# Five pairs of the convolution's input projection as seven half-size products, with their block sums on VectorE and later splitting of the early weight pieces

## The chip, the cores and the metric

One core of a Trainium2 chip runs the kernel. The metric is the device time of one execution in microseconds (us), taken as the median of repeated runs; lower is better.

## The reference

A decoder trunk on 512 tokens of width 1024, with one layer of each of two kinds. What the change touches is the first mixer, ahead of everything else:

```python
def short_conv_mixer(h, w_in, conv_w, w_out):
    b_gate, c_gate, u = jnp.split(h @ w_in, 3, axis=-1)   # h: 512 x 1024, w_in: 1024 x 3072
    v = c_gate * u
    vp = jnp.pad(v, ((0, 0), (CONV_WIDTH - 1, 0), (0, 0)))
    conv = sum(conv_w[k] * vp[:, k:k + S] for k in range(CONV_WIDTH))
    return (b_gate * conv) @ w_out                        # w_out: 1024 x 1024
```

Behind it come a squared-ReLU MLP (1024 to 4096 and back), a shared key/value side, sparse attention, a second MLP and a last RMS norm.

## The kernel before

Everything is float32 outside and float16 in the matrix products: each operand is split into a high half and a low half (`whi`, `wlo` for weights, `x_98` or `xs` for activations), and a product is three matmuls, high by high, low by high and high by low, all added up in PSUM. Activations lie with their 1024 channels on partitions, as eight chunks of 128 x 512 tokens.

Weights stream in as pieces of 128 x 1024 values. SP issues the load into one of three `wst` buffers, ACT writes `whi`, DVE writes `wlo`, each into one of four buffers, and TensorE (PE) uses them some microseconds later. `convert_piece` does this in the order of the list `pieces`; `ahead` keeps a given number of pieces converted before they are used.

The input projection goes in four groups p of 256 channels. In each group three parts (the gate c, the values u, the gate b, as `pc`, `pu`, `pb`) are one pair each: two PSUM banks of 128 x 512, eight chunks, three terms, so 48 matmuls of 512 columns, done by `pair`. PSUM has two banks each of `a`, `b` and `c`; pairs take them in turn as a,b then b,c then c,a. Behind each pair DVE and ACT make `cv_t`, `cv_v`, `cv_o` and `cv_b` of it and at last the convolution's output `y`, again as two halves. The output projection is four more pairs on `y`, each followed by the residual `X`, its sum of squares `ssacc` and the next input `xs`.

Some weights that attention needs much later are split during this stage: `split_some` loads a piece as `pre_in`, makes both halves as `pre_hl`, and SP stores them to DRAM as `early`. There are 14 such pieces, one for each pair from the second group on until all are done.

The whole stage, from the first load to the last output pair, is recorded first and then issued by a planner (`Plan`): a list scheduler that gives each engine a fixed order by its own estimates. On the chip every engine works through its order one by one and waits where an operand is not there; so an instruction that waits holds back all that stand behind it on its engine. Behind the stage comes the MLP, which already uses the seven-product form in its second projection: a 2 x 2 block product with seven block products in place of eight, on sums of blocks (`W_SUMS` for the weights, `R_SUMS` for the activations, `PRODUCTS` for the pairs of blocks). Helper lines L241 (the planned stages) and L275 (the MLPs) stand for nearly all instructions in the profile, so that they are told apart by their tiles.

Of the kernel before, what the change touches and what calls it, by code (L numbers as in the profile page):

```python
# [10 lines left out]
F32 = mybir.dt.float32  # L11
# [269 lines left out]
def body(ctx, tc, x, rel_bias, norm_mix, norm_mlp, mlp_w1, mlp_w2, a_w_in, a_conv_w, a_w_out,  # L281
# [42 lines left out]
    def up_pair(w, m):  # L324

        v = w.rearrange("(c p) (j m n) -> p c j m n", p=128, j=2, n=128)
        for k in (0, 4):
            pieces.append((v[:, k:k + 4, :, m, :], (4, 256), SW))

    def down_blocks(w, p, half):  # L330

        v = w.rearrange("(j c p) n -> c p j n", j=2, p=128)
        for c in range(8 * half, 8 * half + 8, 2):
            pieces.append(([v[c + k, :, :, p * 256:(p + 1) * 256] for k in range(2)], None, SW2))
# [11 lines left out]
            cols(w, c0, 256, scale, k, 4)  # L346


    v = a_w_in[0].rearrange("(c p) (s n) -> c p s n", p=128, s=3)
    for c in range(8):  # L350
        pieces.append((v[c, :, :, 0:256], (3, 256), SW))
    for p in range(1, 4):
        for part in (1, 2, 0):
            block(a_w_in[0], part * D + p * 256)
    for p in range(4):
        block(a_w_out[0], p * 256)
    mlp_pieces(0)
# [3 lines left out]
    CMPS = [(55, 0, 0), (58, 0, 1), (61, 0, 2), (62, 0, 3), (77, 1, 0), (78, 1, 1), (85, 1, 3), (89, 1, 2)]  # L361
    LEAD_IN = ["k0", "q0"]

    RATE = 1
    PRE = ["raw1", "phi0", "q2", "cmp", "q3"]
    early, early_out = [], {}

# [25 lines left out]
    mlp_pieces(1)  # L393

    NS, NW, AHEAD = 3, 4, 2
    NS2, NW2, AHEAD2, PIECE2 = 3, 4, 3, 2048


    W_SUMS = ((OP.add, 4, 0, 2), (OP.subtract, 5, 4, 1), (OP.subtract, 6, 1, 0), (OP.subtract, 7, 3, 5))
# [9 lines left out]
    def load_piece(first=None):  # L409
        i = pos["dma"]  # L410
        if i >= len(pieces):
            return
        if i in early:
            pos["dma"] += 1
            return
        src, shape, _ = pieces[i]
        if shape is None:
            t = wk[0].tile([128, PIECE2], F32, name="wst2", bufs=NS2)
            for k, u in enumerate(src):
                SPQ.dma_start(t[:, k * PIECE:k * PIECE + 512].rearrange("p (j n) -> p j n", j=2), u)  # L420
        else:
            t = wpool.tile([128, PIECE], F32, name="wst", bufs=NS)
            a, n = shape
            v = t[:, :a * n].rearrange("p (a n) -> p a n", a=a)
            if len(src.shape) == 4:
                v = v.rearrange("p a (j n) -> p a j n", j=2)
                for j in range(2):
                    SPQ.dma_start(v[:, :, j], src[:, :, j])
            elif first:
                for k in (1, 2, 0):  # L430
                    (first if k == 1 else SPQ).dma_start(v[:, k], src[:, k])
            else:
                SPQ.dma_start(v, src)
        staged[i] = t
        pos["dma"] += 1

    def convert_piece(step=1024):
# [12 lines left out]
            yield  # L450
        elif shape is None:
            b = t.rearrange("p (k b n) -> p k b n", k=2, n=128)
            with tc.issue_after(root_op[0].ins):
                for e, o, x, y in W_SUMS:
                    DVE.tensor_tensor(b[:, :, o], b[:, :, x], b[:, :, y], op=e)
            hi, lo = (wk[0].tile([128, 2, 7, 128], F16, name=n, bufs=NW2) for n in ("whi2", "wlo2"))
            ACT.activation(hi, b[:, :, 1:], AF.Copy, scale=sc)
            DVE.scalar_tensor_tensor(lo, b[:, :, 1:], sc, hi, op0=OP.mult, op1=OP.subtract)
            ready[i] = (hi, lo)
            yield  # L460
        else:
# [10 lines left out]
            ready[i] = (r(hi), r(lo))  # L472
        while pos["dma"] < len(pieces):
            like = [j for j in range(pos["cv"], pos["dma"]) if blocked(j) == blocked(pos["dma"]) and j not in early]
            if len(like) >= (NS2 if blocked(pos["dma"]) else NS):
                break
            load_piece()

# [18 lines left out]
                pass  # L497
        return ready.pop(i)

    def ahead(far=AHEAD2):  # L500
        while pos["cv"] < len(pieces) and pos["cv"] < pos["use"] + (far if blocked(pos["cv"]) else AHEAD):
            yield from convert_piece()

    def drain(gen):
# [174 lines left out]
    def x_rstd():  # L679
        ss0 = work.tile([128, 4], F32, name="ss0")  # L680
        for t in range(4):
            junk = wk[0].tile([128, D], F32, name="junk", bufs=1)
            ACT.activation(junk, xt[t], AF.Square, accum_out=ss0[:, t:t + 1])
        return rstd_of(ss0)


    ys = new_split(wk[0], "y")
    for p in range(4):
        pc, pu, pb = [], [], []
        if p == 0:  # L690
# [35 lines left out]
            rb2 = ftile("rb2", 1)  # L726
            DVE.tensor_tensor(rb2, rby, rby, op=OP.mult)
            ws = [next_piece(), next_piece()]
        if p == 1:
            ext = wk[0].tile([H, EXT], F32, name="ext")  # L730
            POOL.memset(ext[:, 0:PAD], NEG)
# [7 lines left out]
            for i in range(2):  # L739
                PE.transpose(pp[:, i * 16:(i + 1) * 16], pe_in[:, i], ident[0:16, 0:16])  # L740
            ACT.activation(pet.rearrange("p a b -> p (a b)"), pp[:, 0:32], AF.Copy)
        for dst in (pc, pu, pb):
            if p:
                dst += [acc(), acc()]
                pair(xs, dst)
            else:
                for k in range(2):
                    first_pairs(dst, ws[k], 6 + k)
            drain(ahead())
            split_some(RATE if p else 0)  # L750
# [928 lines left out]
```

## Time and profile before

| | |
|---|---|
| median of 3 runs | 1102.13 us (1101.77 to 1102.78) |
| the profiled execution's own time | 1103.79 us |
| its span, first to last instruction | 1102.0 us |
| granted TensorE clock, mean | 0.999 |
| input projection, second to fourth group | 44.7 to 137.9 us |
| output projection | 137.9 to 179.3 us |
| first MLP begins | 179.4 us |

The profile is one execution. Busy time of an engine is the time in which an instruction ran on it; for PE, matmuls overlap in the pipeline, so their rate is read from the distance of their starts and not from their length. A row of the timeline gives the start, the length, the engine, the line, what it writes and reads, and in brackets the idle time ahead of it with what ended it.

### The profile page before, as it was taken

What the parts mean: (1) busy time and instruction counts of PE and PEld (TensorE: products, weight loads), DVE (VectorE), ACT (ScalarE), POOL (GpSimd) and SP (SyncE); (2) the same over time, 40 slices, a digit from 0 to 9 for tenths busy, and PEclk for the clock granted to TensorE, in tenths of its full rate; (3) what the DMA queues carried; (4) which work ended last, traced back from release to release, by engine and by line L of the source; (5) the groups of instructions that cost most, each with busy time, mean ns of one, the idle gap of its engine ahead of it and who ended that gap; (6) DMA issues with size and microseconds to landing.
All of it is one profiled execution on the core that took longest, in us unless ns stands there. A gap on an engine that the chain in (4) does not pass through costs nothing.

```text
span 1102.0 us, 20132 instructions
## 1 busy us (share of the span) xinstructions
PE 1088.4 (99%) x8009; PEld 696.0 (63%) x8009; DVE 864.5 (78%) x1594; ACT 564.7 (51%) x892; POOL 60.2 (5%) x89
## 2 busy tenths in 40 slices
PE   9999999999999999999999999999999999999997
PEld 4444444446885447885856686675444788444897
DVE  5977466986898776979677779997898799865776
ACT  6544244644333444527666677865655434343353
POOL 1000000000000000000011022211000000000021
PEclk9999999999999999999999999999999999999999
DMA  7897335543333332304424361002753333330232
GB/s 239 283 310 246 112 99 153 153 128 90 119 105 115 115 96 75 99 20 143 139 80 134 78 206 64 21 21 58 208 156 110 108 109 116 115 96 1 77 97 78
DMA packets 155615, 131.37 MB, mean 119 GB/s; under 512 B 8332, under 2 KB 147296, under 8 KB 155520
## 3 DMA queue, kind: packets, MB, share of 16 engines
q1 hardware_dynamic: 152672, 124.74, 37.0%
q10 hardware_dynamic: 2464, 4.70, 1.3%
q8 instruction: 63, 1.03, 0.4%
q0 software_dynamic: 384, 0.63, 0.2%
q14 instruction: 32, 0.26, 0.1%
HBM read 117.56 MB, written 9.48 MB: 115 GB/s over the span
## 4 chain that ended last, share of the span: by engine, by line
PE 93%; DVE 3%; ACT 1%; DMA 1%; issue 1%; POOL 0%; SPq 0%; POOLq 0%; DVEq 0%; ACTq 0%
PE c L275 19%; PE b L275 17%; PE a L241 16%; PE a L275 15%; PE c L241 9%; PE b L241 9%; PE d L275 4%; PE d L241 2%; PE e L275 2%; DVE at_s L241 1%; PE e L241 1%; DVE at_pl L241 0%; DMA whi<-early 0%; ACT xq L241 0%; DMA wst<-a_w_in_dram 0%
## 5 line engine op out<-in xcount | busy, mean ns | idle before, releaser
L275 PEld LDWEIGHTS <-whi 128*128 128x128 f16 x2784 | 272.4, 98 | 139.9 <-issue 0.2
L275 ACT ACTIVATE whi<-wst 128x1024 f16<-128x1024 f32 (+1 forms) x126 | 173.2, 1380 | 199.0 <-PE b L275 70.5
L275 DVE SCALAR_TENSOR_TENSOR wlo<-wst,whi 128x1024 f16<-128x1024 f32 (+1 forms) x126 | 204.3, 1624 | 17.0 <-ACT whi L275 16.6
L275 PEld LDWEIGHTS <-wlo 128*128 128x128 f16 x1392 | 136.2, 98 | 70.8
L241 PEld LDWEIGHTS <-whi 128*128 128x128 f16 x1024 | 97.3, 98 | 96.0 <-issue 2.7
L275 PE MATMUL b<-xs,whi 128*128 128x512 f16 x384 | 114.3, 379 | 0.0
L275 PE MATMUL c<-xs,whi 128*128 128x512 f16 x384 | 114.2, 379 | 0.0
L275 DVE TENSOR_TENSOR wst<-wst 128x256 f32<-128x256 f32 x256 | 95.9, 420 | 21.6 <-DMA wst<-mlp_w_dram 20.5
L275 DVE TENSOR_TENSOR rl<-ml_z,rh 128x1792 f16<-128x1792 f32 x32 | 64.7, 2023 | 43.7 <-ACT rh L275 43.7
L241 ACT ACTIVATE whi<-wst 128x512 f16<-128x512 f32 (+5 forms) x85 | 63.4, 765 | 69.0 <-PE a L241 19.2
L241 DVE SCALAR_TENSOR_TENSOR wlo<-wst,whi 128x512 f16<-128x512 f32 (+5 forms) x85 | 72.3, 863 | 23.4 <-ACT whi L241 23.2
L241 ACT ACTIVATE at_p<-at_s,at_m 128x128 f32<-128x128 f32 (+3 forms) x128 | 71.1, 556 | 35.5 <-DVE at_m L241 33.8
L241 PEld LDWEIGHTS <-wlo 128*128 128x128 f16 x512 | 50.2, 98 | 51.5
L275 ACT ACTIVATE rh<-ml_z 128x1792 f16<-128x1792 f32 x32 | 54.3, 1696 | 54.5 <-DVE ml_z L275 54.5
L275 PE MATMUL a<-xs,whi 128*128 128x512 f16 x256 | 76.1, 379 | 0.0
L275 PE MATMUL c<-xs,wlo 128*128 128x512 f16 x192 | 72.8, 379 | 0.0
L275 PE MATMUL b<-xs,wlo 128*128 128x512 f16 x192 | 72.8, 379 | 0.0
L241 DVE CUSTOM_DVE_ANT_0 at_s<-b,T 128x128 f32<-128x128 f32 (+3 forms) x128 | 59.3, 485 | 16.5 <-PE b L241 15.6
L275 PE MATMUL a<-rh,wlo 128*128 128x256 f16 x256 | 69.1, 273 | 0.0
L275 PE MATMUL a<-rh,whi 128*128 128x256 f16 x256 | 69.1, 273 | 0.0
L275 PE MATMUL a<-rl,whi 128*128 128x256 f16 x256 | 67.8, 273 | 0.0
L275 PE MATMUL c<-rh,wlo 128*128 128x256 f16 x248 | 67.6, 273 | 0.0
(264 smaller groups left out, 2173.7 us busy)
## 6 DMA issues: line engine op xcount, KB each, us to landing
wst<-mlp_w_dram SPq DMA_DIRECT2D x256, 256.0 KB, 3.5
wst<-a_w_in_dram SPq DMA_DIRECT2D x18, 512.0 KB, 6.0
early<-pre_hl SPq DMA_DIRECT2D x14, 512.0 KB, 4.8
wst<-w_kv_dram SPq DMA_DIRECT2D x10, 512.0 KB, 3.7
T<-ext_d ACTq DMA_DIRECT2D x4, 1056.0 KB, 7.0
wst<-a_w_out_dram SPq DMA_DIRECT2D x8, 512.0 KB, 3.5
wst<-b_w_o_dram SPq DMA_DIRECT2D x8, 512.0 KB, 3.8
whi<-early SPq DMA_DIRECT2D x14, 256.0 KB, 3.6
```

Of the source, the lines that this page charges most:

```text
L241: getattr(self.engines[t["e"]], t["op"])(*t["args"], **t["kw"])
L275: return real(*args, **kwargs)
```

## The change

The pairs (group, part) in `SEVEN` (part 1 is `pc`, 2 is `pu`, 0 is `pb`) are computed by a new function `seven`. It views the 1024 x 256 weights and the 1024 x 512 activations as 2 x 2 blocks, and makes seven products of four chunks, three terms and 256 columns each: 84 matmuls of 256 columns in place of 48 of 512. It needs:

- weight pieces in the two-chunk form `wst2` (two buffers), four `W_SUMS` additions of 256 values each, and a split of seven blocks, 2 x 896 values, in place of 1024;
- sums of blocks of the activations, once for all five pairs (`block_sums`, four calls, tiles `sv_z` and the new `xs` in this stage);
- the combination of the seven products in three PSUM banks: ACT copies product 0 from bank `a` to bank `b` as a start for further products there, and copies two partial sums to `sv_p` and `sv_u`; DVE adds these (`sv_d<-c`, `sv_d<-b`), ACT copies the other two halves of `sv_d`. The operations that used to read a pair from PSUM read `sv_d`.

The early pieces are recorded in other places: one behind pair (2, 0), and three, three, four and the rest behind the four output pairs (`PACE`, `PACE_OUT`). `y` now lies in the buffer of `xt`, and the squares of the input go to the `pre_in` buffers. The settings for the MLPs' blocks stay as they were.

```diff
+    SEVEN = [(2, 1), (2, 0), (3, 1), (3, 2), (3, 0)]
...
-            block(a_w_in[0], part * D + p * 256)
+            (seven_blocks if (p, part) in SEVEN else block)(a_w_in[0], part * D + p * 256)
...
-    RATE = 1
+    PACE = {(2, 0): 1}
+    PACE_OUT = [3, 3, 4, 99]
+    SUM_AT = {(0, 0): (0,), (1, 1): (1,), (1, 2): (2, 3,)}
...
+    AHEAD2 = {(SW, False): AHEAD, (SW, True): 2, (SW2, True): 3}
+    NS2 = {SW: 2, SW2: 3}
...
-            ACT.activation(hi, b[:, :, 1:], AF.Copy, scale=sc)
-            DVE.scalar_tensor_tensor(lo, b[:, :, 1:], sc, hi, op0=OP.mult, op1=OP.subtract)
+            for k in [slice(n, n + 1) for n in range(2)] if sc == SW else [slice(0, 2)]:
+                ACT.activation(hi[:, k], b[:, k, 1:], AF.Copy, scale=sc)
+                DVE.scalar_tensor_tensor(lo[:, k], b[:, k, 1:], sc, hi[:, k], op0=OP.mult, op1=OP.subtract)
...
+    def block_sums(c):
+        z = wk[0].tile([128, 8, 256], F32, name="sv_z", bufs=1)
+        for k in range(2):
+            g = vec[:, gain["mix0"] + 2 * c + k:gain["mix0"] + 2 * c + k + 1]
+            ACT.activation(z[:, 2 * k:2 * k + 2].rearrange("p a n -> p (a n)"), X[:, 2 * c + k], AF.Copy, scale=g)
+        for e, o, a, b in R_SUMS:
+            DVE.tensor_tensor(z[:, o], z[:, a], z[:, b], op=e)
+        ACT.activation(sums[:, 0, c], z[:, 4:8], AF.Copy)
+        DVE.tensor_tensor(sums[:, 1, c], z[:, 4:8], sums[:, 0, c], op=OP.subtract)
+
+    def seven(d):
+        X_, W_, V_ = (bank(g)[:, 0:256] for g in "abc")
+        ws = [next_piece(), next_piece()]
+        cv = ahead()
+
+        def product(i, ps, more=False):
+            a, b = PRODUCTS[i]
+            for c in range(4):
+                wh, wl = (u[:, c % 2, a - 1] for u in ws[c // 2])
+                xh, xl = (block_of(hl, c, b) for hl in range(2))
+                PE.matmul(ps, wh, xh, start=c == 0 and not more, stop=False, skip_group_check=more)
+                PE.matmul(ps, wl, xh, start=False, stop=False, skip_group_check=more)
+                PE.matmul(ps, wh, xl, start=False, stop=c == 3, skip_group_check=more)
+
+        u2, u5 = (wk[0].tile([128, 256], F32, name=n, bufs=1) for n in ("sv_u", "sv_p"))
+        lo, hi = slice(0, 256), slice(256, 512)
+        product(0, X_)
+        ACT.activation(W_, X_, AF.Copy)
+        product(4, V_)
+        ACT.activation(u5, V_, AF.Copy)
+        next(cv, None)
+        product(2, W_, True)
+        ACT.activation(u2, W_, AF.Copy)
+        product(5, V_, True)
+        DVE.tensor_tensor(d[:, 1, lo], V_, u2, op=OP.add)
+        next(cv, None)
+        product(3, W_, True)
+        DVE.tensor_tensor(d[:, 0, lo], W_, u5, op=OP.add)
+        product(1, X_, True)
+        ACT.activation(d[:, 1, hi], X_, AF.Copy)
+        drain(cv)
+        product(6, W_, True)
+        ACT.activation(d[:, 0, hi], W_, AF.Copy)
...
+            if (p, part) in SEVEN:
+                d = wk[0].tile([128, 2, S], F32, name="sv_d", bufs=2)
+                seven(d)
+                dst += [d[:, 0], d[:, 1]]
...
-            split_some(RATE if p else 0)
+            split_some(PACE.get((p, part), 0))
+            for c in SUM_AT.get((p, part), ()):
+                block_sums(c)
...
-        split_some(RATE if p < 3 else 99)
+        split_some(PACE_OUT[p])
```

The first place is PE in the fourth group. Before, a pair there runs as matmuls of 512 columns over two banks (`x_98` is the split input):

```order
L241 LDWEIGHTS whi
L241 MATMUL c<-x_98,whi 128x512
L241 LDWEIGHTS wlo
L241 MATMUL c<-x_98,wlo 128x512
L241 LDWEIGHTS whi
L241 MATMUL b<-x_98,whi 128x512
```

Now pair (3, 1) stands there as products of 256 columns; `whi_209` and `whi_212` are its own two weight pieces, `whi_223` is the first of the next pair (3, 2), and `xs` are the block sums of the activations:

```order
L241 MATMUL c<-xs,wlo_213 128x256
L241 LDWEIGHTS whi_212
L241 MATMUL c<-xs,whi_212 128x256
L241 LDWEIGHTS whi_223
L241 MATMUL a<-x_98,whi_223 128x256
L241 LDWEIGHTS whi_209
L241 MATMUL b<-xs,whi_209 128x256
L241 LDWEIGHTS wlo_210
L241 MATMUL b<-xs,wlo_210 128x256
```

The matmuls are of half the width, and the planner put one of the next pair between product 4 (bank `c`) and product 2 (bank `b`, which waits for ACT's copy).

The second place is DVE from the end of the third group on. Before, `cv_b` and `y` of that group were followed by one weight split for each half pair:

```order
L241 TENSOR_TENSOR cv_b<-c,rb 128x512
L241 TENSOR_TENSOR cv_b<-cv_b,cv_o 128x512
L241 TENSOR_TENSOR cv_b<-a,rb 128x512
L241 TENSOR_TENSOR cv_b<-cv_b,cv_o 128x512
L241 TENSOR_TENSOR y<-cv_b,y 128x512
L241 SCALAR_TENSOR_TENSOR wlo<-wst,whi 128x1024
L241 TENSOR_TENSOR y<-cv_b,y 128x512
L241 SCALAR_TENSOR_TENSOR wlo<-wst,whi 128x1024
L241 SCALAR_TENSOR_TENSOR cv_t<-a,rb_137 128x512
L241 SCALAR_TENSOR_TENSOR cv_t<-b,rb_137 128x512
L241 SCALAR_TENSOR_TENSOR wlo<-wst,whi 128x1024 x2
```

Now one `pre_hl` split stands first, and then these (`xt` is `y` in its new buffer, `wst_211` and `wst_214` are the weights of pair (3, 2)); the last of them releases bank `b` to product 6 of pair (3, 1):

```order
L241 TENSOR_TENSOR cv_b<-sv_d,rb 128x512
L241 TENSOR_TENSOR cv_b<-cv_b,cv_o 128x512
L241 SCALAR_TENSOR_TENSOR wlo_224<-wst_211,whi_223 128x896
L241 TENSOR_TENSOR cv_b<-sv_d,rb 128x512
L241 TENSOR_TENSOR cv_b<-cv_b,cv_o 128x512
L241 TENSOR_TENSOR xt<-cv_b,xt 128x512
L241 SCALAR_TENSOR_TENSOR wlo_224<-wst_211,whi_223 128x896
L241 TENSOR_TENSOR xt<-cv_b,xt 128x512
L241 SCALAR_TENSOR_TENSOR wlo_227<-wst_214,whi_226 128x896
L241 TENSOR_TENSOR sv_d<-c,sv_u 128x256
L241 SCALAR_TENSOR_TENSOR wlo_227<-wst_214,whi_226 128x896
L241 TENSOR_TENSOR sv_d<-b,sv_p 128x256
```

Four splits of 896 and two additions of `sv_d` have come between, and PE now waits for the last row.

The third place is DVE right behind it, during pair (3, 2), up to the addition that releases its product 6 (`wst_225` and `wst_228` are the weights of the last pair, (3, 0)):

```order
L241 SCALAR_TENSOR_TENSOR pre_hl<-pre_in,pre_hl 128x1024
L241 SCALAR_TENSOR_TENSOR cv_t<-sv_d,rb_137 128x512
L241 TENSOR_TENSOR wst_225<-wst_225 128x2x128
L241 SCALAR_TENSOR_TENSOR cv_t<-sv_d,rb_137 128x512
L241 TENSOR_TENSOR wst_225<-wst_225 128x2x128 x3
L241 TENSOR_TENSOR wst_228<-wst_228 128x2x128 x3
L241 SCALAR_TENSOR_TENSOR wlo_238<-wst_225,whi_237 128x896
L241 TENSOR_TENSOR wst_228<-wst_228 128x2x128
L241 SCALAR_TENSOR_TENSOR wlo_238<-wst_225,whi_237 128x896
L241 TENSOR_TENSOR sv_d<-c,sv_u 128x256
L241 SCALAR_TENSOR_TENSOR wlo_240<-wst_228,whi_239 128x896 x2
L241 TENSOR_TENSOR sv_d<-b,sv_p 128x256
```

Before, DVE had there two `cv_t` and two splits of 1024 and nothing else, as the last rows of the fence of before show; now it has sixteen instructions.

More of the change, by code (lines that the diff above doesn't have):

```diff
@@ L328, in up_pair, with seven_blocks @@
             pieces.append((v[:, k:k + 4, :, m, :], (4, 256), SW))
+    def seven_blocks(w, c0):
+        v = w.rearrange("(c j p) n -> c p j n", j=2, p=128)
+        for c in (0, 2):
+            pieces.append(([v[c + k, :, :, c0:c0 + 256] for k in range(2)], None, SW))
     def down_blocks(w, p, half):
@@ L395, in body @@
     NS, NW, AHEAD = 3, 4, 2
-    NS2, NW2, AHEAD2, PIECE2 = 3, 4, 3, 2048
+    NW2, PIECE2 = 4, 2048
+    AHEAD2 = {(SW, False): AHEAD, (SW, True): 2, (SW2, True): 3}
+    NS2 = {SW: 2, SW2: 3}
     W_SUMS = ((OP.add, 4, 0, 2), (OP.subtract, 5, 4, 1), (OP.subtract, 6, 1, 0), (OP.subtract, 7, 3, 5))
@@ L415, in load_piece @@
             return
-        src, shape, _ = pieces[i]
+        src, shape, sc = pieces[i]
         if shape is None:
-            t = wk[0].tile([128, PIECE2], F32, name="wst2", bufs=NS2)
+            t = wk[0].tile([128, PIECE2], F32, name="wst2", bufs=NS2[pieces[i][2]])
             for k, u in enumerate(src):
@@ L452, in convert_piece @@
             b = t.rearrange("p (k b n) -> p k b n", k=2, n=128)
-            with tc.issue_after(root_op[0].ins):
+            with nullcontext() if plan.active else tc.issue_after(root_op[0].ins):
                 for e, o, x, y in W_SUMS:
@@ L474, in convert_piece @@
             like = [j for j in range(pos["cv"], pos["dma"]) if blocked(j) == blocked(pos["dma"]) and j not in early]
-            if len(like) >= (NS2 if blocked(pos["dma"]) else NS):
+            if len(like) >= (NS2[pieces[pos["dma"]][2]] if blocked(pos["dma"]) else NS):
                 break
@@ L498, in next_piece, with ahead @@
         return ready.pop(i)
-    def ahead(far=AHEAD2):
-        while pos["cv"] < len(pieces) and pos["cv"] < pos["use"] + (far if blocked(pos["cv"]) else AHEAD):
+    def ahead():
+        while pos["cv"] < len(pieces) and pos["cv"] < pos["use"] + AHEAD2[pieces[pos["cv"]][2], blocked(pos["cv"])]:
             yield from convert_piece()
@@ L681, in x_rstd, with block_of @@
         for t in range(4):
-            junk = wk[0].tile([128, D], F32, name="junk", bufs=1)
+            junk = wk[0].tile([128, D], F32, name="pre_in", bufs=2)
             ACT.activation(junk, xt[t], AF.Square, accum_out=ss0[:, t:t + 1])
         return rstd_of(ss0)
-    ys = new_split(wk[0], "y")
+    def block_of(hl, c, b):
+        if b < 4:
+            return xs[hl][:, 2 * c + b // 2, (b % 2) * 256:(b % 2) * 256 + 256]
+        return sums[:, hl, c, b - 4]
+    def block_sums(c):
[7 more added lines that the diff above has]
+        DVE.tensor_tensor(sums[:, 1, c], z[:, 4:8], sums[:, 0, c], op=OP.subtract)
@@ L688, in body @@
+    sums = work.tile([128, 2, 4, 4, 256], F16, name="xs")
+    ys = None
     for p in range(4):
@@ L728, in body @@
             ws = [next_piece(), next_piece()]
+            ys = new_split(wk[0], "xt")
         if p == 1:
@@ L741, in body @@
             ACT.activation(pet.rearrange("p a b -> p (a b)"), pp[:, 0:32], AF.Copy)
-        for dst in (pc, pu, pb):
-            if p:
+        for part, dst in ((1, pc), (2, pu), (0, pb)):
+            if (p, part) in SEVEN:
+                d = wk[0].tile([128, 2, S], F32, name="sv_d", bufs=2)
+                seven(d)
+                dst += [d[:, 0], d[:, 1]]
+            elif p:
                 dst += [acc(), acc()]
```

## The prediction

> **What bounds the kernel now.** First the page, its busy times and the chain that ended last:
>
> ```profile
> PE 1088.4 (99%) x8009; PEld 696.0 (63%) x8009; DVE 864.5 (78%) x1594; ACT 564.7 (51%) x892; POOL 60.2 (5%) x89
> PE 93%; DVE 3%; ACT 1%; DMA 1%; issue 1%; POOL 0%; SPq 0%; POOLq 0%; DVEq 0%; ACTq 0%
> ```
>
> 93% of the chain is PE. A busy PE can still be a slow one, so the next view is what PE waited for in the first 265 us, which hold the stage that is changed:
>
> ```profile
> PE c L241 <- DVE any L241: 1.3, 1, 1.3
> PE a L241 <- ACT x L241: 0.3, 1, 0.3
> ```
>
> Both are at the start. After 7 us PE waits for nothing, so each microsecond of matmul removed is gained, until something else is late. The windows say what has room: second group, third and fourth, output projection, first MLP up (columns: PE, weight loads, DVE, ACT, POOL, clock, DMA share, GB/s):
>
> ```profile
> 44.70:75.80 31.10, 31.10 (x146) 14.14 (x146) 24.34 (x33) 14.93 (x18) 0.00 (x0) 1.00 0.81 268
> 75.80:137.90 62.10, 62.10 (x289) 28.18 (x288) 39.14 (x49) 21.55 (x24) 0.00 (x0) 1.00 0.59 193
> 137.90:179.30 41.40, 41.40 (x194) 18.76 (x192) 24.73 (x32) 16.65 (x22) 0.00 (x0) 1.00 0.34 101
> 179.30:262.00 82.70, 82.70 (x391) 38.26 (x390) 71.54 (x104) 44.59 (x39) 1.02 (x1) 1.00 0.48 141
> ```
>
> DVE has 23 us free in 75.8 to 137.9 and 16.7 us in the output projection. It is the engine to watch.
>
> **The change: matmuls.** From the timeline of PE, the first matmul of the second pair of group 1 and the first of the third; then two in the MLP's seven-product form that are 84 apart; and the weight loads there:
>
> ```profile
> 55.11 0.38 PE L241 MATMUL b<-x,whi 128*128 128x512 f16 x1
> 65.47 0.38 PE L241 MATMUL c<-x,whi 128*128 128x512 f16 x1
> ...
> 266.04 0.27 PE L275 MATMUL a<-rh,wlo 128*128 128x256 f16 x1
> 275.21 0.27 PE L275 MATMUL a<-rh,wlo 128*128 128x256 f16 x1
> ...
> L275 PEld LDWEIGHTS <-whi 128*128 128x128 f16 x135 | 13.2, 98 | 2.1
> ```
>
> A pair of 48 takes 65.47 - 55.11 = 10.36 us (216 ns each); 84 half-size ones take 275.21 - 266.04 = 9.17 us (109 ns each). One pair gains 1.19 us, five gain 5.95 us. The half-size form has 84 weight loads of 98 ns, 8.2 us, still below 9.17, so they stay hidden.
>
> Here a rule speaks against the change. The Trainium skill (TensorE: Matmul & The Clock Gate, "Back-to-back issue gap") gives for a stream of weight load and matmul pairs some 81 ns at 128 columns and 131 ns at 512. Read straight between these, 256 columns would take an estimated 98 ns, and five pairs would lose 5 x (84 x 0.098 - 48 x 0.131) = 9.7 us. The trace disagrees: 109 and 216 ns, both in streams where each matmul has its own load. By that page's other formula, N / 2.4 + 2.5 ns, the trace agrees.
>
> **The change: DVE between two releases.** Within a pair, product 6 adds to bank `b` only after DVE's `sv_d<-b` has read it, and DVE works in order. So from one `sv_d<-b` to the next DVE must get through all that stands between, while PE needs 9.17 us. What one instruction takes in a row of others is the distance of starts, from the timeline of DVE:
>
> ```profile
> 31.64 0.95 DVE L241 SCALAR_TENSOR_TENSOR wlo<-wst,whi 128x768 f16<-128x768 f32 x1
> 32.50 0.68 DVE L241 COPY X<-d 128x512 f32<-128x512 f32 x1
> ...
> 39.32 0.69 DVE L241 SCALAR_TENSOR_TENSOR cv_t<-a,rb 128x512 f32<-128x512 f32 x1
> ...
> 68.01 0.68 DVE L241 TENSOR_TENSOR cv_v<-b,cv_t 128x512 f32<-128x512 f32 x1
> 68.61 0.68 DVE L241 TENSOR_TENSOR cv_v<-c,cv_t 128x512 f32<-128x512 f32 x1
> 69.21 1.22 DVE L241 SCALAR_TENSOR_TENSOR wlo<-wst,whi 128x1024 f16<-128x1024 f32 x1
> 70.34 2.98 DVE L241 SCALAR_TENSOR_TENSOR cv_o<-cv_v,vec,cv_o 128x512 f32<-128x512 f32 x4
> 73.27 0.18 DVE L241 MEMSET cv_v<- 128x2 f32 x2
> 76.89 0.68 DVE L241 TENSOR_TENSOR cv_b<-c,rb 128x512 f32<-128x512 f32 x1
> 77.61 0.69 DVE L241 TENSOR_TENSOR cv_b<-cv_b,cv_o 128x512 f32<-128x512 f32 x1
> 190.03 2.44 DVE L275 TENSOR_TENSOR wst<-wst 128x256 f32<-128x256 f32 x7 [0.31 <-DMA wst<-mlp_w_dram]
> ```
>
> That is 0.60 for 512 elements, 0.72 where the next one needs the result, 1.13 for a split of 1024, 0.86 for 768 (so about 1.0 for the new 896), 0.73 for one `cv_o`, 0.34 for 256. The sums over the order's rows:
>
> - Up to the first, of (2, 1): 70 instructions from group 1's `cv_t` on, 31 of them the new sums, splits and `sv_d` of the first two pairs, make 43.3 us. `cv_t` starts at 39.3 us as before; 82.6. PE begins the pair at 65.47 + 10.36 = 75.8 and needs bank `b` after six products, at 83.7. It just holds; I take 0.3, at most 1.5, since any wait of DVE on the way adds to it.
> - (2, 1) to (2, 0), with the unchanged pair between them: 19.1 us against 9.17 + 10.36 = 19.5. Nothing.
> - (2, 0) to (3, 1): one `pre_hl` 1.13, two `cv_b` couples 2.65, four splits 4.0, two of `y` 1.2, two `sv_d` 0.68: 9.65 us, 0.5 over.
> - (3, 1) to (3, 2): `pre_hl` 1.13, two `cv_t` 1.2, eight weight sums 2.7, four splits 4.0, two `sv_d` 0.68: 9.7 us, 0.55 over.
> - (3, 2) to (3, 0): 7.1 us. Nothing.
>
> So 0.3 + 0.5 + 0.55 = 1.35 us. With the full lengths of the rows, 0.08 more for each of the 13 and 17 instructions of the two middle ones, and 1.5 in the first, it would be 5.0.
>
> **The change: ACT's copies.** The trace has no 256-column copy from PSUM; the nearest rows (ACT by form):
>
> ```profile
> L241 ACT ACTIVATE pre_hl<-pre_in 128x1024 f16<-128x1024 f32 x14 | 14.7, 1053 | 21.0 <-DMA pre_in<-phi_v_w_dram 7.6 <-DMA pre_in<-b_w_qg_dram 6.9 <-DMA pre_in<-phi_k_w_dram 6.5
> ...
> L241 ACT ACTIVATE whi<-wst 128x768 f16<-128x768 f32 x7 | 5.8, 838 | 5.6 <-DMA wst<-a_w_in_dram 4.2 <-DVE pre_hl L241 1.4
> ...
> L241 ACT ACTIVATE x<-d,vec 128x512 f16<-128x512 f32 x4 | 2.7, 678 | 0.9 <-PE d L241 0.9
> ...
> L241 ACT ACTIVATE whi<-wst 128x256 f16<-128x256 f32 x3 | 1.2, 412 | 2.7 <-DMA wst<-a_w_in_dram 2.7
> ```
>
> So 0.41 to 0.68 us, nearer the first since the size is the same. Each copy is covered by one product of PE, 9.17 / 7 = 1.31 us. It is late only where a split (0.9 for 896, between 0.41 and 0.84 and the 1.05 of 1024) or a `cv_o` copy is ahead of it on ACT. I take 0.3 us over all five pairs, between 0 and 1.5 (one copy in each pair late by 0.3).
>
> **The change: loads.** The two `wst2` buffers can be loaded again only when DVE has split them. Landings after the issue, in the busy first 60 us and in the quiet 100 to 175 us, and the length of one issue on SP there (ns):
>
> ```profile
> wst<-a_w_in_dram SPq DMA_DIRECT2D x9, 512.0 KB, 7.5
> ...
> wst<-a_w_out_dram SPq DMA_DIRECT2D x8, 512.0 KB, 3.5
> ...
> L241 SPq DMA_DIRECT2D wst<-a_w_out_dram x8: 367/368/368, 111.0 to 145.6; - x8
> ```
>
> With early pieces gone from the third and fourth groups, 3.5 us is the nearer. The loop of one buffer is then 0.4 to issue the second half, 3.5 to land, 1.35 for four sums, 2.0 for two splits: 7.2 us of the 9.17. It fits, but DVE stands still in order when a load is not there just then; for five such loads I add 0.65 us, between 0 and 1.5.
>
> **The change: moved work.** `block_sums` is four times 4 x 0.34 + about 1.13, some 10 us on DVE, about what nine `pre_hl` took that leave the first two groups; from `cv_t` on it is in the 43.3 us. At the start the first sums stand ahead of a split that PE waits for soon (timelines; the last row is the last read of the input `xt`):
>
> ```profile
> 21.36 0.96 DVE L241 SCALAR_TENSOR_TENSOR wlo<-wst,whi 128x768 f16<-128x768 f32 x1
> 22.73 0.38 PE L241 MATMUL a<-x,wlo 128*128 128x512 f16 x1
> ...
> 22.17 0.19 ACT L241 ACTIVATION_READ_ACCUMULATOR junk<-xt 128x1 f32 x1
> ```
>
> The split is done 0.4 us early. The two loads ahead of it on SP are of the same bytes as the two `pre_in` loads that stood there; I take 0, at most 1 us. In the output projection there are now eight `pre_hl`: 9 us on DVE of 16.7 free, 8.4 on ACT of 24.8 free, and 8 x 1 MB (half a MB in and out each) in 41 us over the 101 GB/s, about 300 GB/s. Before, ten went through SP, ACT and DVE between these two (timeline of DVE):
>
> ```profile
> 52.19 1.22 DVE L241 SCALAR_TENSOR_TENSOR pre_hl<-pre_in,pre_hl 128x1024 f16<-128x1024 f32 x1
> 95.71 1.23 DVE L241 SCALAR_TENSOR_TENSOR pre_hl<-pre_in,pre_hl 128x1024 f16<-128x1024 f32 x1 [2.04 <-ACT pre_hl L241]
> ```
>
> 43.5 / 9 = 4.8 us each; eight need 38.7 of the 41.4 us. The last stands ahead of the last pair's `X` on DVE, for which the MLP's first bank waits. It fits by 2.7 us; nothing is charged. `y` in the place of `xt` waits for reads that end at 22.4 us; nothing.
>
> **The sum.** 5.95 gained, 1.35 + 0.3 + 0.65 = 2.3 lost: 3.65 us. The profiled execution took 1103.79 (its span of 1102.0 and 1.8 around it), so 1100.1; it lies 1.66 above the median, and against the median of 1102.13 the forecast is 1098.5. Bounds: no loss at all gives 1096.2; all upper ones together, 5.0 + 1.5 + 1.5 + 1.0 = 9.0, give 1105.2.
>
> **Rivals.** A measurement of this kernel tells 0.2%, 2.2 us, from no change.
>
> 1. The saving is eaten. DVE goes by its upper bound, 5.0, and ACT and the loads cost what I took: 5.0 + 0.95 = 5.95 lost, nothing gained, 1102.1. For it: from the end of the second group to the last `y` DVE has 94 instructions, 59.2 us by the distances above, and PE, without any loss, gives it 5 x 9.17 + 10.36 and the 9 us until the last chunk of `y` is used, 65. Against it: those distances are measured in such rows. Chance 0.20.
> 2. Slower: the two-buffer loop of `wst2` becomes the bound. If loads land in 7.5 us there too, the loop takes 11.2 us, 2.05 over the 9.17 of a pair, in each of the last three pairs: 6.15 us on top of the 2.3, less 5.95, so 1104.6. To lose more than the forecast gains it must be over by 1.2 us a pair, a landing of 6.7 us. For it: the 7.5 of the first 60 us. Against it: those were with a DMA share of 0.8 and more, and the load that made it has moved away. Chance 0.08.
> 3. Slower: half-size products are bound by their weight loads. 36 more loads of 98 ns a pair, not hidden, are 17.6 us, less 5.95: 1113.8. The 109 ns speak against it. Chance 0.01. The rule of the Trainium skill that is told above (TensorE: Matmul & The Clock Gate, "Back-to-back issue gap") points this way.
> 4. The early pieces overrun the output projection. At 5.6 us each, eight take 44.8, 3.4 over, and the MLP starts that much later: 1101.9. Against it: in the rows above it was 4.8 under heavier traffic. Chance 0.06.
>
> The forecast keeps 0.65. Faster by over 0.2% means below 1099.9: 0.65. Within 0.2%: rivals 1 and 4, 0.26. Slower: rivals 2 and 3, 0.09. To leave out no more than 2 in 10, the range goes from the case without loss, 1096.2, past most of rivals 1 and 4, to 1102.2.
>
> **What would show it.** In the profile after: PE waits between 80 and 135 us for DVE `sv_d` and ACT copies, together about 2.3 us, each under 1 us; the fourth group's PE at 109 ns a matmul; the MLP starting near 179.4 - 3.65 = 175.8 us; all later stages unchanged and moved. It is wrong if PE waits more than 4 us in that stage, if DVE's idle time there ends mostly on `wst` loads, or if the MLP's first pair waits for `X`.

## The result and the profile after

The changed kernel takes 1095.55 us, the median of 4 runs (1095.13 to 1096.60), against 1102.22 (1101.77 to 1102.78) for the kernel before beside it: a ratio of 0.9941, with a 95% interval of 0.9923 to 0.9958. Two later sets of runs gave 0.9939 (0.9927 to 0.9952) and 0.9941 (0.9924 to 0.9957). It is faster, as forecast, but by 6.7 us instead of 3.65, and so 0.65 us below the range. The profiled execution took 1096.60, its span 1094.8 us; before it was 1103.79 and 1102.0.

The page of after, busy times and chain:

```profile
PE 1081.8 (99%) x8189; PEld 712.7 (65%) x8189; DVE 899.5 (82%) x1674; ACT 588.3 (54%) x939; POOL 60.0 (5%) x89
PE 90%; DVE 5%; DMA 2%; ACT 2%; issue 1%; POOL 0%; SPq 0%; POOLq 0%; DVEq 0%; ACTq 0%
```

PE has 180 matmuls more (5 x 36) and is busy 6.6 us less. What it waited for in the first 262 us, longer waits only:

```profile
PE c L241 <- DVE any L241: 1.3, 1, 1.3
PE b L241 <- DVE sv_d L241: 0.7, 1, 0.7
PE a L241 <- ACT x L241: 0.5, 1, 0.5
```

One wait is new, 0.7 us for `sv_d`. The windows, cut as in the prediction but at the times of after:

```profile
44.70:75.80 31.10, 31.10 (x150) 14.44 (x148) 30.64 (x49) 16.93 (x21) 0.00 (x0) 1.00 0.51 154
75.80:131.90 56.10, 55.42 (x460) 44.69 (x458) 53.60 (x87) 30.10 (x51) 0.00 (x0) 1.00 0.54 171
131.90:173.30 41.40, 41.40 (x196) 18.95 (x194) 32.27 (x38) 24.07 (x30) 0.00 (x0) 1.00 0.93 296
```

DVE is busy 30.64 of 31.10 us in the second group and 53.60 of 56.10 in the next two, where it was 24.34 and 39.14 (of 62.1). It is as full as the forecast said. Where it stood still, and when it released bank `b` (timeline of DVE, pairs (2, 0), (3, 1), (3, 2), (3, 0)):

```profile
94.73 0.69 DVE L241 TENSOR_TENSOR cv_v<-b,cv_t 128x512 f32<-128x512 f32 x1
96.89 0.88 DVE L241 TENSOR_TENSOR wst<-wst 128x256 f32<-128x256 f32 x2 [1.47 <-DMA wst<-a_w_in_dram]
...
102.74 0.42 DVE L241 TENSOR_TENSOR sv_d<-b,sv_p 128x256 f32<-128x256 f32 x1
...
112.41 0.42 DVE L241 TENSOR_TENSOR sv_d<-b,sv_p 128x256 f32<-128x256 f32 x1
...
122.23 0.42 DVE L241 TENSOR_TENSOR sv_d<-b,sv_p 128x256 f32<-128x256 f32 x1
...
129.89 0.43 DVE L241 TENSOR_TENSOR sv_d<-b,sv_p 128x256 f32<-128x256 f32 x1 [0.44 <-PE b L241]
```

From release to release are 9.67 and 9.82 us; the prediction had 9.65 and 9.7. PE at two of them, product 6 of (2, 0) and of (3, 2), each beginning with `b<-xs`:

```profile
102.29 0.27 PE L241 MATMUL a<-x,whi 128*128 128x256 f16 x1
103.21 0.27 PE L241 MATMUL b<-xs,whi 128*128 128x256 f16 x1 [0.65 <-DVE sv_d L241]
...
122.59 0.27 PE L241 MATMUL a<-x,wlo 128*128 128x256 f16 x1
122.70 0.27 PE L241 MATMUL b<-xs,whi 128*128 128x256 f16 x1
```

At (2, 0) PE lost 0.92 - 0.11 = 0.81 us. At (3, 2) DVE was late too, but PE lost nothing: the rows ahead, `a<-x`, end with eight matmuls of the next pair (3, 0). At product 6 of (3, 1), with one such matmul ahead, PE lost 0.07 us. The third loss, 0.2 us, is at product 2 of (3, 1), where ACT's copy (second row) stood behind a weight split:

```profile
106.19 0.93 ACT L241 ACTIVATE whi<-wst 128x896 f16<-128x896 f32 x1
107.03 0.36 ACT L241 ACTIVATE b<-a 128x256 f32<-128x256 f32 x1
```

To see where the time came from, the span is cut at five matmuls that both kernels have: the last one ahead of the `e<-onehot` product (start of the second group), and the 7000th, 4000th, 3000th and last from the end (in the first MLP, at attention's beginning, behind attention's early loads, and the end). In us:

| part | before | after | difference |
|---|---|---|---|
| start | 43.25 | 42.42 | -0.83 |
| stage, to the first MLP | 175.92 | 170.99 | -4.93 |
| MLP and what follows | 393.05 | 393.05 | 0 |
| attention with its early loads | 85.25 | 84.29 | -0.96 |
| to the last matmul | 397.92 | 397.91 | 0 |
| tail, behind the last matmul | 6.57 | 6.11 | -0.46 |

The stage gained 4.93. The other 2.25 us came in three places that the diff doesn't touch.

### The profile page after: what moved, and what is told of

The parts are those of the page before. It is cut to its first block, busy times and chain, and to the rows that moved or that the text cites. A ratio compares the mean times of both kernels' runs of the same rounds, so it can differ in the third digit from the quotient of the medians.

```text
span 1094.8 us, 20636 instructions
## 1 busy us (share of the span) xinstructions
PE 1081.8 (99%) x8189; PEld 712.7 (65%) x8189; DVE 899.5 (82%) x1674; ACT 588.3 (54%) x939; POOL 60.0 (5%) x89
## 3 DMA queue, kind: packets, MB, share of 16 engines
q8 instruction: 64, 1.05, 0.4%
## 4 chain that ended last, share of the span: by engine, by line
PE 90%; DVE 5%; DMA 2%; ACT 2%; issue 1%; POOL 0%; SPq 0%; POOLq 0%; DVEq 0%; ACTq 0%
PE c L275 19%; PE b L275 17%; PE a L275 15%; PE a L241 14%; PE c L241 8%; PE b L241 8%; PE d L275 4%; PE d L241 2%; PE e L275 2%; DMA wst<-a_w_in_dram 1%; DVE wlo L241 1%; DVE at_s L241 1%; DMA whi<-early 1%; PE e L241 1%; DVE at_pl L241 0%
## 5 line engine op out<-in xcount | busy, mean ns | idle before, releaser
L275 PEld LDWEIGHTS <-whi 128*128 128x128 f16 x2784 | 272.5, 98 | 139.7
L275 PEld LDWEIGHTS <-wlo 128*128 128x128 f16 x1392 | 136.2, 98 | 70.8
L241 PEld LDWEIGHTS <-whi 128*128 128x128 f16 x1144 | 108.7, 98 | 78.6 <-issue 1.8
L241 ACT ACTIVATE whi<-wst 128x512 f16<-128x512 f32 (+6 forms) x95 | 70.8, 771 | 37.4 <-PE c L241 8.7
L241 DVE SCALAR_TENSOR_TENSOR wlo<-wst,whi 128x512 f16<-128x512 f32 (+6 forms) x95 | 81.2, 872 | 11.3 <-ACT whi L241 11.1
L241 PEld LDWEIGHTS <-wlo 128*128 128x128 f16 x572 | 55.9, 98 | 45.3 <-issue 1.0
```

The lines of the kernel that those rows point to most:

```text
L241: getattr(self.engines[t["e"]], t["op"])(*t["args"], **t["kw"])
L275: return real(*args, **kwargs)
```

## The experiments

Theory A: the stage gives about 5 us, because the matmuls that the planner put from the next pair into PE's order hide DVE's overrun, and the rest is chance of single executions. Theory B: the rest is made by the change, through its moves. A third theory came up on the way.

**The same kernels again.** No edit; `before_again`, `before_third`, `after_again`, `after_third`, `after_fourth`.

> The kernel before, profiled a second time. Theory A (about 5 us of the gain are made by the change, in the stage itself; the other 1.7 to 2 us of the difference of the two profiles are chance of single executions: the clock's first step up at the start, one wait for an early weight load near 657 us): of the three places, at least one reads differently from the first profile of before: the second group's third pair ends elsewhere than 75.8 us, or the 1.3 us wait for an early load near 657 us is gone. Theory B (the change itself makes those parts, through other traffic and another phase): this profile repeats the first one, 75.8 us and the 1.3 us wait, within 0.1 us.

> The changed kernel, profiled a second time and timed in five rounds. Both theories expect the stage from the first half-size product to the MLP's start to take 98.75 us again, with the stalls of 0.8 and 0.2 us at pairs (2, 0) and (3, 1). A: the start (75.00 us) or the place near 657 us may read differently; the median of many runs, in which chance evens out, is 5 to 6.5 us under the kernel before. B: start and the place near 657 us repeat, and the ratio stays at 0.9940.

> The kernel before, a third profile, read in five parts: start, stage, the MLP and the part up to attention, attention with its early loads, and the tail behind the last matmul. Stage 175.92 us and tail 6.57 again under both theories. Theory A (start and attention are chance): the start lies anywhere between 41.6 and 43.5 us, and attention anywhere between 84.0 and 85.3. Theory B (attention is slower in the order of before): attention 84.4 to 85.3 again.

> The changed kernel, a third profile. Stage 170.2 to 171.1 us (the stall at (2, 0) between 0 and 0.9, by when one load lands), tail 6.11. Theory A: attention anywhere between 84.0 and 85.3. Theory B: 84.05 to 84.3 again.

| | start | stage | attention | tail |
|---|---|---|---|---|
| before_again | 42.56 | 175.92 | 84.41 | 6.56 |
| before_third | 42.80 | 175.92 | 84.68 | 6.58 |
| after_again | 41.60 | 171.10 | 84.06 | 6.12 |
| after_fourth | 42.03 | 171.43 | 84.12 | 6.12 |

(The expectation of `after_fourth` stands with the last runs; its stage lies over the 171.1 expected there, with a stall of 1.13 us at (2, 0). `after_third` was one execution of 6516 us, told of at the end.) The start differs from run to run: the first two matmuls of 512 columns that come 0.216 us apart, instead of 0.427, are elsewhere in each profile. The trace's record of the clock steps up 10.35, 5.24 and 5.56 us after the first instruction in the three profiles of before, and after 6.45, 5.83 and 3.97 us in those of after. At nearly the same step, 10.35 in the first of before and 10.75 in `only_third` (below), which has the changed start, it ends at 43.25 and 43.45: no gain there. PE also waited 0.69 and 0.76 us for the input's load `xt` in the second and third profile of before and in none of after; but `no_filler` (below), with the changed start, waited 0.58 us for it. Attention, on the other hand, is slower in each profile of before than in each of after, and the tail is the same to 0.02 within a kernel. The wait for the early load near 657 us was 1.3, 0.4 and 0.7 us in the three profiles of before: chance sets its size, but not that it is there. So A is wrong about these two parts: as a whole they are no chance.

**The moves alone.**

```diff
-    SEVEN = [(2, 1), (2, 0), (3, 1), (3, 2), (3, 0)]
+    SEVEN = []
-    SUM_AT = {(0, 0): (0,), (1, 1): (1,), (1, 2): (2, 3,)}
+    SUM_AT = {}
```

> No pair as seven products and no block sums; early pieces, y in the input's buffer and the squares in the pre_in buffers as in the changed kernel. A: PE is not short of anything in this stage before the change, so moving alone gives nothing there: 1102.2, within 0.7 us. B: the moves take the early stores and loads out of the way and give the part that the matmuls don't explain: 1100.3 to 1100.7, 1.5 to 2 us under the kernel before.

1102.49, ratio 0.9995 (0.9986 to 1.0004); stage 175.92, attention 85.25, tail 6.86. The moves give nothing. It speaks against B as it was stated.

**The old pace.**

```diff
-    PACE = {(2, 0): 1}
-    PACE_OUT = [3, 3, 4, 99]
+    PACE = {(p, k): 1 for p in (1, 2, 3) for k in (0, 1, 2)}
+    PACE_OUT = [1, 1, 1, 99]
```

> The five pairs with the early pieces at their old places in the record, one behind each pair. Between the releases VectorE then has 18.4, 9.9, 9.7 and 8.2 us instead of 19.0, 9.65, 9.7 and 7.1, and seven early splits of 1.13 ahead of and within the third group instead of one. Theory A: the later splitting is worth little, 0 to 1 us: 1095.6 to 1096.8. Rival (the pairs only pay because the early pieces left VectorE): seven splits of 1.13 that aren't hidden, up to 7.9 us, 1100 and more.

1096.17, ratio 0.9946 (0.9933 to 0.9960), stage 171.22: as fast as the changed kernel within the interval. Its losses lie elsewhere, 0.46 and 0.74 us at product 2 of (2, 1) and of (2, 0), where PE waits for ACT's copy. The planner finds room for the early splits either way; the later splitting isn't what pays.

**No matmuls of the next pair.** `held_back` holds the last matmul of product 6 of the pair before. `no_next_pair` has all of this, `no_filler` all but the lines on product 4.

```diff
-        product(0, X_)
+        with plan.behind(*held_back):
+            product(0, X_)
-        product(4, V_)
+        with plan.behind(*held_back):
+            product(4, V_)
-        product(6, W_, True)
+        held_back[:] = [product(6, W_, True)]
```

> As the changed kernel, but product 0 of a seven-product pair is held behind the last product of the pair before it, so that the order of PE can't put matmuls of the next pair where PE would wait for VectorE's addition. Theory A (VectorE is over its time by 0.5 to 0.65 us in two pairs as forecast, and the fillers hide it): PE stalls 0.2 us more at (3, 1) and about 0.9 us at (3, 2), the MLP starts 1.0 to 1.1 us later and the time is 1096.6. Rival (VectorE's overrun was never real, because its instructions follow each other faster than the sums of rows say): no stall over 0.2 us, 1095.6.

> As no_filler, with product 4 held back too, since in no_filler the planner put the next pair's product 4 where its product 0 had been: in its trace nine matmuls of product 4 stand ahead of the products 6 of pairs (3, 1) and (3, 2), and the time hardly moved. Theory A (VectorE is over its time as forecast and matmuls of the next pair hide it): without any of the next pair's matmuls PE stalls 9 x 0.109 = 1.0 us more than in no_filler, nearly all of it at product 6 of (3, 2); from the end of the start phase to the MLP it takes 171.3 us where no_filler took 170.3, and the time is about 1097. Rival (there is no overrun to hide): the 170.3 us stay, 1096.0.

`no_filler`: 1096.03, ratio 0.9943 (0.9930 to 0.9955), stage 170.27. It missed, because nine matmuls of product 4 took the places of those of product 0. It lost only 0.07 us at (2, 0): there DVE waited 0.71 us for the load, not 1.47. `no_next_pair`: 1096.18, ratio 0.9947 (0.9934 to 0.9959), 0.8 us under the time expected; stage 171.25, 0.98 us more than `no_filler`, about the 1.0 expected. PE at product 6 of (3, 2):

```profile
120.97 0.27 PE L241 MATMUL a<-x,whi 128*128 128x256 f16 x1
121.08 0.59 PE L241 MATMUL c<-xt,whi 128*128 128x512 f16 x2
121.51 0.38 PE L241 MATMUL c<-xt,wlo 128*128 128x512 f16 x1
121.72 0.38 PE L241 MATMUL c<-xt,whi 128*128 128x512 f16 x1
122.32 0.27 PE L241 MATMUL b<-xs,whi 128*128 128x256 f16 x1 [0.22 <-DVE sv_d L241]
```

Now the planner took four matmuls of the output projection (`c<-xt`, 0.86 us) as cover. In the distances of starts (0.216 us behind a matmul of 512 columns, 0.109 behind one of 256, where nothing is late), PE lost 0.38 here, 0.19 at product 6 and 0.30 at product 2 of (3, 1), 0.10 at product 2 of (3, 0), and 0.38 at (2, 0), which is the load again. `no_filler` had lost 0.07, 0.20 and 0.07 at product 6 and product 2 of (3, 1) and at (2, 0), and at most 0.03 in the other two places. So the 0.98 us hit the expected sum in part by luck: nearly all was to come at product 6 of (3, 2), and 0.38 came there; 0.31 are the load. What shows the mechanism is the single place: product 6 was ready at 121.08 and let in at 122.32, DVE is 1.24 us late, and PE loses what the 0.86 us of cover leave of it. The times of the runs can't tell these kernels apart; the traces do.

**Three pairs, and six.**

```diff
-    SEVEN = [(2, 1), (2, 0), (3, 1), (3, 2), (3, 0)]
+    SEVEN = [(3, 1), (3, 2), (3, 0)]
```

That is `only_third`; and `six_pairs`:

```diff
-    SEVEN = [(2, 1), (2, 0), (3, 1), (3, 2), (3, 0)]
+    SEVEN = [(2, 1), (2, 2), (2, 0), (3, 1), (3, 2), (3, 0)]
```

> Only the three pairs of the fourth group as seven products; sums, pace and buffers as in the changed kernel. Theory A (1.19 us for each pair, and stalls only by chance of a load): the stage takes 175.9 - 3 x 1.19 = 172.35 us with at most 0.4 of stalls; time 1098.2 to 1098.8. Theory B (part of the gain is fixed and comes with the moves, not with the pairs): as much as the changed kernel less 2 x 1.0, below 1097.8.

> Pair (2, 2) as seven products too. By the same distances of rows VectorE has 9.3, 9.5, 12.4, 10.9 and 10.2 us between the six releases of bank b, where PE needs 9.17 each: 6.4 us over. Theory A (VectorE's order is the limit, and matmuls of the next pair hide about 1 us of it): 1.19 gained, some 5 lost, stalls of 2 to 3 us at pairs (2, 0), (3, 1) and (3, 2); the time is 1098 to 1100. Rival (VectorE has room, the forecast's rows overstate it): 1.2 us faster than the changed kernel, 1094.4.

`only_third`: 1099.66, ratio 0.9980 (0.9971 to 0.9988), stage 173.92: 0.9 us over A's upper figure, and far from B's. One stall explains nearly all of it, at (3, 1): 1.54 us from the start before, 112.24, where 0.11 are usual, so 1.43 lost. PE's row, and then ACT's:

```profile
113.78 0.27 PE L241 MATMUL b<-xs,whi 128*128 128x256 f16 x1 [1.27 <-ACT sv_u L241]
```

```profile
112.40 1.06 ACT L241 ACTIVATE pre_hl<-pre_in 128x1024 f16<-128x1024 f32 x1 [1.54 <-DMA pre_in<-phi_v_w_dram]
113.36 0.36 ACT L241 ACTIVATE sv_u<-b 128x256 f32<-128x256 f32 x1
```

ACT stood idle for the load of an early piece (by chance 1.54 us too), with the copy `sv_u` that PE needed queued behind it. Without that, 173.92 - 1.43 = 172.49, near 175.92 - 3.57 = 172.35, and a wait for `sv_d` at product 6 of (3, 2) lost the 0.14 between: 1.19 us for each pair holds.

`six_pairs`: 1101.67, ratio 0.9995 (0.9986 to 1.0004), stage 175.68, only 0.24 under before: the sixth pair gives back nearly all that five gained. Its waits of PE between 70 and 170 us:

```profile
PE a L241 <- DVE wlo L241: 2.2, 4, 1.0
PE b L241 <- ACT b L241: 1.9, 4, 0.8
PE b L241 <- DVE sv_d L241: 0.4, 1, 0.4
```

I expected 1098 to 1100, so the loss was undersized, and its place was wrong as well. DVE was busy 54.48 of the 56 us from 75 to 131. By the distances of starts PE lost 3.0 us to DVE's weight splits, 2.5 to ACT's copies and 0.8 to `sv_d`.

**The shift alone, without the change.** The kernel before, with the term `w[0], xs[1]` left out for chunks 1, 3 and 5 of the five pairs:

```diff
-        PE.matmul(ps, w[0], xs[1], start=False, stop=False)
+        if not less[0]:
+            PE.matmul(ps, w[0], xs[1], start=False, stop=False)
```

> The kernel before, with six of the 48 matmuls left out in each of the pairs (2, 1), (2, 0), (3, 1), (3, 2) and (3, 0): high weights by low activations, for three of the eight chunks. That is 30 x 0.216 = 6.5 us less for PE, and nothing added. Theory A (PE bounds the stage, VectorE, ScalarE and the loads of before would keep up, and what is gained here moves all that follows): stage 169.4 us, time 1095.6 to 1096.1. If the shift alone brings the faster attention and the shorter tail: attention near 84.2, tail near 6.1, and 1094.5. Rival (something else is nearly as late as PE): a stage over 170.5 and 1097 or more.

1094.68, ratio 0.9933 (0.9920 to 0.9947). The stage took 169.45, exactly 6.47 less: here PE alone is the bound. But attention went to 83.81 and the tail to 6.24, though neither was touched. So the two small parts can come without the pairs and without the moves.

**Sums behind the release.** A planner that reckons 1.5 us more for a `wst2` load:

```diff
-        return self.dma
+        return self.dma + (1500 if ap.tensor.name.startswith("wst2") else 0)
```

> The changed kernel, but the planner reckons 1.5 us more for a wst2 load to land, and so puts the sums of the load that VectorE waited for behind the additions that release bank b of pair (2, 0). Theory A (the stall at (2, 0) is VectorE standing still, in order, for that load): it is gone, the next release comes 10.7 us after the last instead of 9.65 but from an earlier start, and the stage takes 170.0 to 170.6 us instead of 171.0; time about 1095.1. Rival (the load has to be waited for somewhere, and the stall moves to pair (3, 1)): 171.0 us and 1095.6.

Stage 170.05, as expected, and no stall over 0.2 us: DVE's wait for that load is gone, and 175.92 - 170.05 = 5.87 is nearly the full 5.95. The time was 1096.04, ratio 0.9942 (0.9930 to 0.9955): no faster than the changed kernel that the runs could tell. In the changed kernel that stall was 0.8 to 1.1 us in three profiles (in `no_filler`, with the same order up to there, 0.07), so some gain was due. The profile shows where part of it went: attention took 84.56 us, 0.40 over the mean of after. DVE stood 1.10 us there for a load (`T`, from `ext_d`; in after 0.2 to 0.65), and PE then 0.90 us for DVE's `phi_t` (in after up to 0.44). Why that load came later, and whether it did in the other executions, stays open.

**Where the instruction fetches fall.** A row of the page of after, from the part on the DMA queues (transfers, MB, share):

```profile
q8 instruction: 64, 1.05, 0.4%
```

That is 16 KB each, one for 256 of PE's 16378 rows (8189 matmuls with a weight load each). From the first to the last transfer of queue 8 the trace counts 255 rows between two, and the number of transfers goes with that of PE's rows, so they are read here as fetches of PE's instructions. In the kernel before, one falls among the early loads that attention waits for (42.5 to 44.0 us into that part), and one about 0.05 us behind the start of the last matmul, among the last stores. With 360 rows more these places are free. So the change could gain there by the number of its instructions alone, and a few small matmuls with no use must be able to turn it round (52 in `before_shifted`, 76 in `after_shifted`):

```diff
     plan.issue()
+    small = bank("d")
+    for _ in range(52):
+        PE.matmul(small[:, 0:128], xs[0][:, 0, 0:128], xs[0][:, 0, 0:128], start=True, stop=True)
```

> The kernel before, with 52 more small matmuls (128 columns, each with its weight load, result not used) between the output projection and the MLP: 104 rows for TensorE, nothing else. In the traces so far TensorE's instructions are fetched by a transfer on queue 8 about every 256 rows; in the kernel before one falls 42.5 to 44.0 us into the part with attention, beside the early loads for which PE then waits 0.7 to 1.6 us, and one 0.05 us after the last matmul, beside the last store (tail 6.57 us). The changed kernel has 360 rows more, 104 over a whole number of fetches, and neither. Theory C (the change gains about 1.2 us by where the fetches fall): with 104 rows more the kernel before has them where the changed kernel has: the part with attention takes 83.8 to 84.6 us instead of 84.4 to 85.3, the tail 6.1 instead of 6.57. Rival (chance of the loads, or how far the program has come): 84.4 to 85.3 and 6.57 stay.

> The changed kernel, with 76 such matmuls in the same place: 152 rows, which with the 360 of the change are two whole fetches, so that the fetches fall as in the kernel before. Theory C: the wait for the early load 45 us into the part with attention is back (0.7 to 1.6 us, the part takes 84.6 to 85.3 us), and the tail is 6.5 to 6.6. Rival: 84.05 to 84.3 and 6.11 as in the changed kernel.

> The changed kernel once more, since the third profile of it was of one strangely slow execution. Stage 170.2 to 171.1 us, attention 84.0 to 84.4, tail 6.11, and fetches of TensorE's instructions neither between 41.6 and 45.6 us into the part with attention nor behind the last matmul.

| | attention | tail | fetch 41.6 to 45.6 us into attention | fetch behind the last matmul |
|---|---|---|---|---|
| before, three profiles | 84.41 to 85.25 | 6.56 to 6.58 | yes | yes |
| before_shifted | 84.09 | 6.24 | no | no |
| after, three profiles | 84.06 to 84.29 | 6.11, 6.12 | no | no |
| after_shifted | 85.40 | 6.79 | yes | yes |

Both turned round, with sizes a little off the expected ones (tail of `before_shifted` 6.24 for 6.1; `after_shifted` 85.40 for at most 85.3 and 6.79 for at most 6.6). The other programs fit as far as the wait goes: PE waited for the early load 0.4 to 1.4 us in all five profiles with a fetch 42.5 to 44.1 us into attention (the three of before, `moves_only`, `after_shifted`), and at most 0.2 us in the eleven without. The nearest fetches outside, at 41.33 (`sums_later`), 41.49 (`old_pace`) and 45.64 us (`only_third`), made no such wait. The length of the part is not set by this wait alone: `old_pace` (84.86), `six_pairs` (84.71) and `sums_later` (84.56) have no fetch there and are as slow as before, because PE waited 0.7 to 1.0 us for `phi_t` behind the load `T`. Less these two waits of PE, the part has 83.7 to 84.0 us in all sixteen profiles but the first of after (84.29, with neither wait). In the tail, too, `only_third` (6.42) and `six_pairs` (6.48) come near to before without a fetch; what is clear-cut there is the end of the last data packet, 4.76 us behind the start of the last matmul without a fetch and 5.1 to 5.5 with one.

The DMA view of before, first from 653.8 to 657.8 us and then from the last matmul to the end (queue, packets, MB, share; then stores with KB and us from issue to landing):

```profile
q1 hardware_dynamic: 539, 0.78, 64.6%
q8 instruction: 1, 0.02, 1.5%
...
q8 instruction: 1, 0.02, 0.8%
out_dram<-xs SPq DMA_DIRECT2D x1, 512.0 KB, 3.5
out_dram<-xs ACTq DMA_DIRECT2D x1, 256.0 KB, 3.1
```

The same of after (there is no line of queue 8):

```profile
q1 hardware_dynamic: 606, 0.85, 74.3%
...
out_dram<-xs SPq DMA_DIRECT2D x1, 512.0 KB, 2.6
out_dram<-xs ACTq DMA_DIRECT2D x1, 256.0 KB, 2.8
```

And of `after_shifted`:

```profile
q1 hardware_dynamic: 676, 0.92, 77.8%
q8 instruction: 1, 0.02, 1.4%
...
q8 instruction: 1, 0.02, 1.1%
out_dram<-xs SPq DMA_DIRECT2D x1, 512.0 KB, 3.9
out_dram<-xs ACTq DMA_DIRECT2D x1, 256.0 KB, 3.5
```

PE's wait at the early load, between 600 and 700 us, in before and then in `after_shifted`; in after PE itself has none:

```profile
PE a L241 <- DMA whi<-early: 1.3, 1, 1.3
```

```profile
PE a L241 <- DMA whi<-early: 1.4, 1, 1.4
```

The added matmuls took 2.91 and 4.24 us in the traces. Without them `before_shifted` (1104.52, ratio 1.0017, 1.0008 to 1.0026) is at 1101.61, 0.7 under before; `after_shifted` (1101.24, ratio 0.9990, 0.9981 to 0.9999) is at 1097.0, 0.8 over `after_fourth` (1096.22). Each interval is about 1 us to either side, so the times agree in sign but prove little by themselves. What shows the effect is the traces, one of each shifted kernel.

## Why the prediction was wrong

The direction and the main term were right, the size was not: of the 2.3 us of waits that it charged to PE, the profiled execution shows 1.08. By its steps:

- **Matmuls, 5.95 us gained: right.** 84 in 9.17 us, and the stage of `sums_later`, with hardly a stall, is 5.87 shorter. By the prediction's estimate from the rule of the Trainium skill (TensorE: Matmul & The Clock Gate, "Back-to-back issue gap") the pairs would have lost 9.7 us; the traces disagree with it, with 216 ns at 512 columns and 109 at 256.
- **DVE between two releases, 1.35 us lost: this step failed.** Its sums of rows were right to 0.12 us (the second runs over 17 instructions, as the sum has it, not 16), and DVE was late. But the step charged PE with all of DVE's lateness, as if product 6 were the next thing in PE's order. It isn't: the order that stood in the document already showed a matmul of the next pair between two products of (3, 1). Two at (3, 1), with 0.2 us in which PE waited for ACT anyway, and eight at (3, 2) filled the time, and PE lost 0.07 us instead of 1.05. `no_next_pair` and its four output matmuls show the cover at work: with 0.86 us of it against 1.24 of lateness, PE lost 0.38. The first release, 0.3, cost nothing either.
- **Loads, 0.65 lost: about right in size, 0.8 to 1.1.** It was one load of the five, at (2, 0), and not a little of each. Its second half, issued at 92.01, landed 4.8 us later, where the sum took 3.5; the halves of the other four landed after 2.7 to 4.0 us.
- **ACT's copies, 0.3 lost: right,** 0.2, behind a split as described. A copy took 0.36 us, under the lower bound of 0.41.
- **Output projection: right.** The MLP waited for nothing; it began at 173.75.
- **"All later stages unchanged and moved": failed too.** Mean of three profiles each, attention was 0.62 us shorter and the tail 0.46. The neutral shift of the kernel before gave 0.69 and 0.33 of this, by where PE's instruction fetches fall; the other 0.13 us of the tail stays open. The lower end of the range, "no loss at all", rested on this and was no bound.

In all, the stage of after took 171.17 us in the mean of three profiles, 4.75 less than before, where the forecast had 3.65: 1.1 of the 2.95 us that it missed. Attention and the tail are another 1.1, nearly all of it by the fetches. The last 0.75 stays open: the start ended 0.85 earlier in the mean of three profiles, which at the two nearly equal clock steps isn't seen, and the load of the input came late in profiles of both starts. Three profiles of each can't settle whether the change has a part in it.

Of the rivals, the first (the saving eaten by DVE) is what happens in `six_pairs`, one pair further on. The second, the load loop, needed a landing of 6.7 us; the longest of these in after took 4.8. The third was excluded by the spacing. The fourth asked for a wait at the MLP that didn't come.

## What to carry to other kernels

When an engine in strict order waits for another, read what stands in its order just ahead of the wait before charging the lateness: independent work placed there hides it up to its own length. When a change alters the number of instructions, look at the parts it doesn't touch for a microsecond or so, and show by a neutral shift of the instruction count whether they belong to the change. And test one step further: the sixth pair showed that five was near the limit of DVE, which the time of five didn't show.

## What the runs showed of the hardware

- A 16 KB fetch of PE's instructions has a cost where loads or stores that are waited for are under way. Where one fell among attention's early loads, PE waited 0.4 to 1.4 us for one of them, in five profiles of five; elsewhere at most 0.2, in eleven. The last data packet ended 5.1 to 5.5 us behind the start of the last matmul in the same five, which have a fetch there too, and at 4.76 us in the eleven (the execution of 6516 us, told of below, is left out). The Trainium skill (Runtime: NRT & Kernel Launch, "Instruction fetch mechanics") has the sequencer refill in blocks of 16 KiB, 256 instructions, and calls the cost mostly hidden. The traces agree with the block, 256 of PE's rows for each fetch, and show two places where the cost isn't hidden. How a fetch delays the other transfers no run here shows.
- In these sixteen profiles the clock's step to full rate came between 3.97 and 10.75 us after the first instruction, and the start ended between 41.6 and 43.5 us.
- One execution of the changed kernel (`after_third`) took 6516 us. From its page:

```profile
PE 6507.1 (100%) x8189; PEld 2526.6 (39%) x8189; DVE 923.1 (14%) x1674; ACT 601.6 (9%) x939; POOL 59.7 (1%) x89
```

DVE and ACT took 923 and 602 us of work, as usual (900 and 588); PE's matmuls came 1.28 us apart at 512 columns and 0.64 at 256, 5.9 times the usual distance, from beginning to end. No other run of that program did so, and its cause is open.
